# Queries times carried state as one product per head on two row halves, with both heads' outputs in PSUM banks of their own

## The chip, the cores and the metric

The kernel runs on one core of one Trainium2 chip. The core has five engines that run beside each other: TensorE (PE in the profile, its weight loads PEld), VectorE (DVE), ScalarE (ACT), GpSimd (POOL) and SyncE (SP, which issues most transfers). PE writes its results to PSUM, a buffer of eight banks; one bank holds 512 fp32 values on each of 128 partitions. The metric is the device time of one execution in microseconds, lower is better.

## What is computed

One layer of a streaming encoder on 1024 prompt rows and 32 sample rows of width 1024. An input projection feeds two groups of heads, gated linear attention (4 heads, keys of 64, values of 128) and a gMLP; then come an output projection, a normalisation, an MLP of width 4096 with squared ReLU, and a second normalisation. The change lies in the gated attention. The reference computes it block by block, with a matrix state `S` (64 x 128 for each head) that is carried on:

```python
def gla_block(S, q, k, v, g):
    b = jnp.cumsum(g, axis=2)
    o_inter = jnp.einsum('bhid,bhde->bhie', q * jnp.exp(b), S)
    ...
    o = o_inter + jnp.einsum('bhij,bhje->bhie', att, v)
    b_last = b[:, :, -1:, :]
    S_new = jnp.exp(b_last[:, :, 0, :])[..., None] * S + jnp.einsum(
        'bhjd,bhje->bhde', k * jnp.exp(b_last - b), v)
    return S_new, o
...
o = o * lax.rsqrt(jnp.mean(jnp.square(o), axis=-1, keepdims=True) + RMS_EPS) * gla_norm_g.astype(f32)
o_gla = o.reshape(Bn, T, GLA_WIDTH).astype(h.dtype) * jax.nn.silu(r)
```

`o_inter` is the product of queries and carried state that the change touches; everything is in fp32.

## The kernel before

The 1056 rows are cut into three blocks and each block into three windows: eight windows of 128 prompt rows and one of 32 sample rows. The four heads are worked on as two pairs (`Pair`, line 610), one after the other, so 18 windows pass through the attention stage. A pair's two heads lie on top of each other: key dimension of head 0 on partitions 0 to 63, of head 1 on 64 to 127. The state tile `st` (line 615) is 128 x 2 x 128; head 0 fills the rows 0 to 63 of the first 128 columns, head 1 the rows 64 to 127 of the second, and the rest is zero.

For each window, in the generator `gla` (line 860):

- `elem` (line 730) prepares one window ahead the decayed queries and keys, in a tile `zx` of which there are two. POOL, ACT and DVE work on it. The queries that meet the state are `x[:, 3]`.
- `gram` (line 770) multiplies keys and queries in many small products into the PSUM tile `gt` (two banks), transposes the decayed keys (line 793), and puts the masked result into `att`.
- `outp` (line 808) first forms the state's increment (line 817). Then it takes a PSUM tile `o` of one bank, of which there are two in turn (line 819). In its columns 0 to 255 it multiplies queries with the state in one product of 128 rows and 256 columns (line 821; the first window of a pair has none, as its state is zero), and adds `att` times values for each head (line 824). DVE then updates the state (line 830).
- `gla_norm` (line 837) works in two pieces. The first: ACT squares and sums the output (line 844), POOL forms the scale (lines 845 and 846), ACT scales the output into `on` (line 848). The second, due 8000 ns later by the planner's clock (line 849): PE transposes `on` into the columns 256 to 511 of the same `o` (line 851), and DVE multiplies that into `mix` (line 854).

PE's instructions run in the order in which the program writes them (`manual_schedule`, line 104); the other engines' orders are chosen by the framework, which also puts in the waits. The order of writing comes from a planner, `Order` (line 51): generators give back how much PE time a step takes and how long they rest, and the planner takes the stream of the highest priority that is due. `outp` is written, its `gla_norm` is added at priority 0 (line 879) and so its first piece is written at the planner's next step, ahead of the next `gram`, unless an older `gla_norm` is due first. Steps of the projections (`proj_v`, `proj_qk`, `out_proj`, priority 6) fill the time between.

PSUM holds in this stage four banks for `mm` (projections, line 583), two for `gt` and two for `o`: all eight.

Of the kernel before, what the change touches and what calls it, by code (L numbers as in the profile page):

```python
# [10 lines left out]
F32 = mybir.dt.float32  # L11
# [8 lines left out]
P = 128  # L20
# [77 lines left out]
def build(tc, io):  # L98
    nc = tc.nc
    V, S, G, PE, DM = nc.vector, nc.scalar, nc.gpsimd, nc.tensor, nc.sync  # L100
    order = Order()
    ctx = ExitStack()
    with ctx:
# [9 lines left out]
        def mm():  # L113
            return cur["ps"].tile([P, 512], F32, tag="mm", name="mm", bufs=cur["mm"])
# [4 lines left out]
        ident = cst.tile([P, P], F32, name="ident")  # L119
# [6 lines left out]
        def col(name, k, n=1):  # L126
            o = PV[name][0]
            return pv[:, o + k:o + k + n]
# [186 lines left out]
        with tc.tile_pool(name="pa", bufs=1, reuse_waits="tile") as pa, \  # L315
# [36 lines left out]
            for _ in range(3):  # L352
                t = wp.tile([P, 2, 1088], F32, tag="whl", name="wst2", bufs=3)
# [227 lines left out]
        with tc.tile_pool(name="pb", bufs=1, reuse_waits="tile") as pb, \  # L581
# [226 lines left out]
            def outp(pr, b, wi, zx, ak):  # L808
                off, w, c = WIN[b][wi]
                z, x, el = zx  # L810
                att, ks = ak
                vt = pr.v[3 * b + wi]
                st = pr.st[c]
                first = (c == 0 and b == 0 and wi == 0)
                ds = mm()
                for hd in range(2):
                    PE.matmul(ds[64 * hd:64 * hd + 64, :128], ks[:w, 64 * hd:64 * hd + 64],
                              vt[:w, 128 * hd:128 * hd + 128], start=True, stop=True, tile_position=(0, 64 * hd))
                ot = psb.tile([P, 512], F32, tag="o", name="o", bufs=2)
                if not first:  # L820
                    PE.matmul(ot[:w, 0:256], x[:, 3, :w], st.rearrange("p h f -> p (h f)"), start=True, stop=False)
                for hd in range(2):
                    fs_ = slice(128 * hd, 128 * hd + 128)
                    PE.matmul(ot[:w, fs_], att[:w, hd, :w], vt[:w, fs_], start=first, stop=first or hd == 1)
                for hd in range(2):
                    r = slice(64 * hd, 64 * hd + 64)
                    if first:
                        V.tensor_copy(st[r, hd], ds[r, :128])
                    else:
                        V.scalar_tensor_tensor(st[r, hd], st[r, hd], el[r], ds[r, :128], ALU.mult, ALU.add)  # L830
                    if c == 1 or (b == 2 and wi == 1):
                        s0 = 128 * pr.p + 64 * hd
                        DM.dma_start(io["st_s" if c else "st_p"][s0:s0 + 64], st[r, hd])
                pr.out += 1
                return ot

            def gla_norm(pr, b, wi, ot):

                off, w, _ = WIN[b][wi]
                ms = sm.tile([P, 2], F32, tag="ms", name="ms")  # L840
                on = pb.tile([P, 2, 128], F32, tag="on", name="on", bufs=2)
                ov = [ot[:w, 128 * hd:128 * hd + 128] for hd in range(2)]
                for hd in range(2):
                    S.activation(on[:w, hd], ov[hd], AF.Square, accum_out=ms[:w, hd:hd + 1])
                G.tensor_scalar(ms[:w], ms[:w], 1.0 / 128, RMS_EPS, ALU.mult, ALU.add)
                an = [G.tensor_tensor(ms[:w], ms[:w], mhalf[:w].to_broadcast([w, 2]), ALU.pow).ins]
                for hd in range(2):
                    an.append(S.activation(on[:w, hd], ov[hd], AF.Identity, scale=ms[:w, hd:hd + 1]).ins)
                yield 0, 8000
                for hd in range(2):  # L850
                    PE.transpose(ot[:, 256 + 128 * hd:256 + 128 * hd + w], on[:w, hd], ident[:w, :w])
                mx = mix[b][:, 2 * pr.p:2 * pr.p + 2, off:off + w]
                tv = ot[:, 256:512].rearrange("p (h t) -> p h t", h=2)[:, :, :w]
                an.append(V.scalar_tensor_tensor(mx, tv, col("gla_norm_g", 0), mx, ALU.mult, ALU.mult).ins)
                behind[3 * b + wi] = an
                yield 220, 2000
                if wi == 2:
                    pr.normed += 1

            def gla(pr):  # L860
                nxt = None
                for b in range(3):
                    for wi in range(3):
                        if nxt is None:
                            yield lambda: len(pr.dd) >= 1 and len(pr.q) >= 1 and (not pr.p or prs[0].out >= 8)
                            nxt = elem(pr, 0, 0)
                            yield 0, 4000
                        zx = nxt
                        w = WIN[b][wi][1]
                        ak = gram(pr, b, wi, zx)  # L870
                        j = 3 * b + wi + 1
                        yield (1700 if w == 128 else 1700), 200
                        if j < 9:
                            yield lambda: len(pr.dd) > j // 3 and len(pr.q) > j // 3
                            nxt = elem(pr, j // 3, j % 3)
                        yield 0, 3200
                        yield lambda: len(pr.v) >= j
                        ot = outp(pr, b, wi, zx, ak)
                        order.add(gla_norm(pr, b, wi, ot), 0)
                        yield 1300, 0  # L880
# [126 lines left out]
        with tc.tile_pool(name="pd", bufs=1, reuse_waits="tile") as pd, \  # L1007
# [254 lines left out]
            tv = {k: t.rearrange("p (a k n) -> p a k n", a=2, k=2) for k, t in td.items()}  # L1262
# [458 lines left out]
```

## Time and profile before

| what | value |
|---|---|
| time, median of 3 runs | 1234.48 us (1232.83 to 1236.89) |
| the profiled execution's own time | 1231.84 us |
| its span, first to last instruction | 1230.1 us |
| mean granted TensorE clock | 0.979 of full speed |
| PE busy | 1169.0 us, 95% of the span |
| DVE busy | 918.0 us, 75% |
| ACT busy | 528.9 us, 43% |
| POOL busy | 480.6 us, 39% |

Times inside the profile count from the first instruction. The attention stage takes about 256 to 410 us of the span: its first product of `att` and values starts at 256.6 us, its last transposes at 409.3 us. An fp32 product shows as two records, each with its weight load. Rows of the timeline give start, duration, engine, line of the kernel, operation and tiles; where the engine stood idle before a row, brackets give for how long and what ended it. Rows that give windows list, after the stretch and its length, the busy time and number of instructions of PE, PEld, DVE, ACT and POOL, then the granted clock, the share of DMA and GB/s.

### The profile page before, as it was taken

The numbers are of one execution on the slowest core, as the hardware profiler recorded it, in microseconds if no ns is written. First come the engines' busy times: TensorE is split into PE (matmuls) and PEld (weight loads), VectorE is DVE, ScalarE is ACT, GpSimd is POOL, SyncE is SP. The second block draws the span as 40 slices with busy tenths as digits, with TensorE's granted clock in tenths as the row PEclk, the third lists the DMA queues.
The fourth block names the chain that finished last, engine by engine and source line by source line (L and its number), as shares of the span: only waits on it lengthen the run. The fifth ranks groups of instructions, "written<-read, shape, count | busy, mean of one in ns | idle before, by whom it ended". The sixth has DMA issues, their size and how long they took to land.

```text
span 1230.1 us, 22225 instructions
## 1 busy us (share of the span) xinstructions
PE 1169.0 (95%) x8539; PEld 1113.4 (91%) x8539; DVE 918.0 (75%) x1889; ACT 528.9 (43%) x1081; POOL 480.6 (39%) x666
## 2 busy tenths in 40 slices
PE   5999998999899999899989999999999999999994
PEld 3678997988788999789989999999999999999994
DVE  5664797468987688657759769589498696796686
ACT  4462423445555666552435343343443443433221
POOL 3442132246665154358541442334314413432043
PEclk9999998999899999889989999999999999999998
DMA  9631563110102765204762672744825626637412
GB/s 372 240 122 57 194 221 126 35 36 4 39 2 89 263 205 175 101 31 148 267 240 70 206 253 90 256 155 134 300 87 196 242 90 214 227 108 248 141 50 93
DMA packets 49498, 188.46 MB, mean 153 GB/s; under 512 B 5328, under 2 KB 10928, under 8 KB 49392
## 3 DMA queue, kind: packets, MB, share of 16 engines
q1 hardware_dynamic: 35280, 109.97, 25.8%
q0 software_dynamic: 14112, 77.08, 18.2%
q8 instruction: 67, 1.10, 0.4%
q14 instruction: 39, 0.32, 0.1%
HBM read 171.36 MB, written 15.66 MB: 152 GB/s over the span
## 4 chain that ended last, share of the span: by engine, by line
PE 67%; DVE 16%; DMA 5%; POOL 4%; issue 3%; ACT 3%; SPq 0%; POOLq 0%; DVEq 0%; ACTq 0%
PE mm L250 19%; PE mm L1379 15%; PE mm L1446 12%; PE mm L1240 8%; PE mm L284 3%; DVE hl L1043 3%; PE zp L284 2%; DVE jk L903 2%; DMA raw<-in_w_dram 2%; DVE acc L1471 1%; DMA wst<-in_w_dram 1%; DVE wad L903 1%; PE zp L250 1%; DMA tdT<-hl 1%; PE mm L1146 1%
## 5 line engine op out<-in xcount | busy, mean ns | idle before, releaser
L1042 ACT CAST hl<-raw 128x512 fp32r<-128x512 f32 (+1 forms) x238 | 143.8, 613 | 243.5 <-PE mm L1446 95.0
L1043 DVE TENSOR_TENSOR hl<-raw,hl 128x512 fp32r<-128x512 f32 (+1 forms) x238 | 206.0, 871 | 40.7 <-ACT hl L1042 40.7
L1379 PE MATMUL mm<-ring,hl 128*128 128x384 f32 x960 | 173.6, 338 | 3.4 <-DMA ring<-tdT 3.4
L1379 PEld LDWEIGHTS mm<-ring,hl 128*128 128x128 f32 x960 | 168.9, 190 | 3.8 <-issue 3.7
L1446 PE MATMUL mm<-ring,hl 128*128 128x384 f32 x792 | 140.7, 335 | 1.3 <-DVE acc L1471 1.3
L1446 PEld LDWEIGHTS mm<-ring,hl 128*128 128x128 f32 x792 | 137.4, 188 | 1.9 <-ACT ring L1042 1.4
L250 PE MATMUL mm<-hT,whl 128*128 128x384 f32 (+1 forms) x792 | 129.4, 322 | 0.8 <-ACT mix L306 0.8
L250 PEld LDWEIGHTS mm<-hT,whl 128*128 128x128 f32 x792 | 127.0, 188 | 2.2 <-issue 1.1
L250 PE MATMUL mm<-h,hl 128*128 128x288 f32 (+1 forms) x756 | 121.4, 316 | 2.5 <-POOL h L239 2.2
L250 PEld LDWEIGHTS mm<-h,hl 128*128 128x128 f32 x756 | 114.6, 195 | 5.3 <-POOL h L239 4.1
L1087 POOL TENSOR_TENSOR raw<-raw 128x512 f32<-128x512 f32 x26 | 36.3, 1397 | 183.4 <-DMA raw<-in_w_dram 158.8
L1471 DVE SCALAR_TENSOR_TENSOR acc<-mm,G,acc 128x384 f32<-128x384 f32 x162 | 93.6, 606 | 5.3 <-PE mm L1446 4.8
L1240 PE MATMUL mm<-fb,hl 128*128 128x288 f32 x708 | 97.0, 295 | 0.0
L1240 PEld LDWEIGHTS mm<-fb,hl 128*128 128x128 f32 x708 | 95.4, 188 | 0.0
L1251 DVE SCALAR_TENSOR_TENSOR acc<-mm,G,acc 128x256 f32<-128x256 f32 (+3 forms) x176 | 61.6, 389 | 12.2 <-PE mm L1240 12.2
L250 PE MATMUL mm<-mhl,hl 128*128 128x384 f32 (+1 forms) x384 | 63.8, 319 | 2.0 <-ACT hl L1042 1.8
L250 PEld LDWEIGHTS mm<-mhl,hl 128*128 128x128 f32 x384 | 58.8, 188 | 2.6 <-ACT hl L1042 2.1
L1327 POOL DMA_DIRECT2D ring<-tdT x56 | 31.3, 560 | 75.4 <-PE mm L1379 41.3
L284 PE MATMUL mm<-whl,hT 128*128 128x272 f32 (+1 forms) x384 | 54.2, 304 | 5.3 <-DVE whl L637 5.3
L284 PEld LDWEIGHTS mm<-whl,hT 128*128 128x128 f32 x384 | 52.3, 206 | 6.8 <-DVE whl L637 5.5
L284 PE MATMUL zp<-zvw,hT 128*128 128x512 f32 x192 | 53.2, 419 | 4.6 <-ACT hT L236 4.5
L1403 DVE TENSOR_TENSOR tmps<-mm,tmps 128x384 f32<-128x384 f32 x28 | 15.6, 558 | 50.6 <-PE mm L1379 50.6
(255 smaller groups left out, 2246.7 us busy)
## 6 DMA issues: line engine op xcount, KB each, us to landing
ring<-tdT POOLq DMA_DIRECT2D x56, 768.0 KB, 5.7
raw<-in_w_dram SPq DMA_DIRECT2D x80, 512.0 KB, 4.0
ring<-tdB POOLq DMA_DIRECT2D x42, 768.0 KB, 6.3
wst<-in_w_dram SPq DMA_DIRECT2D x34, 512.0 KB, 4.0
wad<-in_w_dram SPq DMA_DIRECT2D x24, 512.0 KB, 4.3
tdT<-hl SPq DMA_DIRECT2D x16, 384.0 KB, 2.7
st<-in_w_dram SPq DMA_DIRECT2D x10, 512.0 KB, 10.2
tdB<-h SPq DMA_DIRECT2D x6, 768.0 KB, 4.5
```

Of the source, the lines that this page charges most:

```text
L250: PE.matmul(pt[:, :n], h[:, a, 128 * kk:128 * kk + 128], act[:, b_, k, :n], start=(i == 0 and j == 0), stop=(i == 7 and j == 2))
L284: PE.matmul(pt[:n, :width], act[:, a, k, off:off + n], hl[:, b_, width * kk:width * kk + width], start=(k == 0 and a + b_ == 0), stop=(k = ...
L903: V.scalar_tensor_tensor(jk, w, 1.0, csb[:, c], ALU.mult, ALU.mult, accum_out=acc_)
L1042: S.copy(hl[:, 0, :n], src)
L1043: V.tensor_tensor(hl[:, 1, :n], src, hl[:, 0, :n].bitcast(F32), ALU.subtract)
L1087: G.tensor_tensor(s, a21, a22, ALU.add)
L1240: PE.matmul(pt[:, :n], hl[kk // 2][:, a, o_:o_ + 128], f(kk)[:, c_], start=(kk == 0 and j == 0), stop=(kk == 3 and j == 2))
L1251: V.scalar_tensor_tensor(ac, pt[:, o + lo - p0:o + hi - p0], G2[:, m, c:c + 1], ac, ALU.mult, ALU.add)
L1327: G.dma_start(s, td[t, j].rearrange("p (a c) -> p a c", a=2))))
L1379: PE.matmul(pt[:, :384], hl[:, a, o_:o_ + 128], quad(ts[j])[:, b_, kk], start=first and j + kk + i == 0, stop=j + kk + i == 4, skip_group_ ...
L1446: PE.matmul(pt[:, :384], hl[:, a, o_:o_ + 128], f[:, b_, kk], start=first and kk + i == 0, stop=kk + i == 3, skip_group_check=True)
L1471: V.scalar_tensor_tensor(ac, v, G2[:, m, 0:1], ac, ALU.mult, ALU.add)
```

## The change

Only `outp` and `gla_norm` change. One PSUM tile `o` of two banks, taken once, serves all 18 windows. Head 0's output lies in its first bank and head 1's in its second. Windows alternate between the left and the right 256 columns of both banks (`half`); of these the first 128 hold the output and the next 128 its transpose. A set, `o_used`, asserts while the program is written that a half is not taken again before its window's second norm piece is written.

The state product becomes one product for each head, of 64 rows and 128 columns: head 0 on the upper row half of the array, head 1 on the lower (`tile_position`), each into its head's bank. The products of `att` and values, the norm's reads and the transposes keep their form and move to the new places.

```diff
-                ot = psb.tile([P, 512], F32, tag="o", name="o", bufs=2)
+                if not o_t:
+                    o_t.append(psb.tile([P, 2, 512], F32, name="o"))
+                half = ocount[0] % 2
+                ocount[0] += 1
+                assert half not in o_used
+                o_used.add(half)
+                ot = o_t[0][:, :, 256 * half:256 * half + 256]
                 if not first:
-                    PE.matmul(ot[:w, 0:256], x[:, 3, :w], st.rearrange("p h f -> p (h f)"), start=True, stop=False)
+                    for hd in range(2):
+                        r = slice(64 * hd, 64 * hd + 64)
+                        PE.matmul(ot[:w, hd, :128], x[r, 3, :w], st[r, hd], start=True, stop=False,
+                                  tile_position=(64 * hd, 0))
                 for hd in range(2):
-                    fs_ = slice(128 * hd, 128 * hd + 128)
-                    PE.matmul(ot[:w, fs_], att[:w, hd, :w], vt[:w, fs_], start=first, stop=first or hd == 1)
+                    PE.matmul(ot[:w, hd, :128], att[:w, hd, :w], vt[:w, 128 * hd:128 * hd + 128], start=first, stop=True)
...
-                return ot
+                return ot, half
...
-                ov = [ot[:w, 128 * hd:128 * hd + 128] for hd in range(2)]
+                ot, half = ot
+                ov = [ot[:w, hd, :128] for hd in range(2)]
...
-                    PE.transpose(ot[:, 256 + 128 * hd:256 + 128 * hd + w], on[:w, hd], ident[:w, :w])
+                    PE.transpose(ot[:, hd, 128:128 + w], on[:w, hd], ident[:w, :w])
                 mx = mix[b][:, 2 * pr.p:2 * pr.p + 2, off:off + w]
-                tv = ot[:, 256:512].rearrange("p (h t) -> p h t", h=2)[:, :, :w]
+                tv = ot[:, :, 128:128 + w]
                 an.append(V.scalar_tensor_tensor(mx, tv, col("gla_norm_g", 0), mx, ALU.mult, ALU.mult).ins)
                 behind[3 * b + wi] = an
+                o_used.remove(half)
```

More of the change, by code (lines that the diff above doesn't have):

```diff
@@ L834, in outp @@
                 pr.out += 1
-                return ot
+                return ot, half
+            o_t, ocount, o_used = [], [0], set()
             def gla_norm(pr, b, wi, ot):
```

## The prediction, made before the changed kernel was run

> **What bounds the kernel now.** I read the page first: the busy digits of TensorE (PE) by slice, the granted clock, and the chain that ended last.
>
> ```profile
> span 1230.1 us, 22225 instructions
> ...
> PE   5999998999899999899989999999999999999994
> ...
> PEclk9999998999899999889989999999999999999998
> ...
> PE 67%; DVE 16%; DMA 5%; POOL 4%; issue 3%; ACT 3%; SPq 0%; POOLq 0%; DVEq 0%; ACTq 0%
> ```
>
> One slice is 30.75 us, so the gated-attention stage, 256 to 410 us, is slices 8 to 13, counted from 0. PE is nearly full there and carries two thirds of the chain. PE's order is written by hand (line 104), so whatever makes PE wait holds back all PE work behind it. Next I read the timeline of one undisturbed cycle, from one window's attention product (L824) to the next one's:
>
> ```profile
> 343.24 0.70 PE L821 MATMUL o<-st,zx 128*128 128x256 f32 x2
> 343.77 0.61 PE L824 MATMUL o<-v,att 128*128 128x128 f32 x4
> 344.02 0.40 POOL L741 TENSOR_TENSOR zx<-b 128x128 f32<-128x128 f32 x1 [10.67 <-PE o L821]
> 344.31 0.46 PE L783 MATMUL gt<-zx 64*32 64x32 f32 x32
> 344.59 0.26 ACT L844 ACTIVATE on<-o 128x128 f32<-128x128 f32 x1
> ...
> 344.99 0.20 ACT L844 ACTIVATION_READ_ACCUMULATOR on<-o 128x1 f32 x1
> ...
> 345.84 0.33 PE L793 MATMUL mm<-ident,zx 128*128 128x128 f32 x1
> 346.01 0.38 PE L851 MATMUL o<-ident,on 128*128 128x128 f32 x2
> 346.14 4.53 PE L284 MATMUL mm<-whl,hT 128*128 128x256 f32 x36
> 346.43 0.48 DVE L854 SCALAR_TENSOR_TENSOR mix<-o,pv,mix 128x256 f32<-128x256 f32 x1
> 346.79 0.29 POOL L749 TENSOR_TENSOR zx<-b 128x64 f32<-128x64 f32 x1
> 347.04 0.46 POOL L764 TENSOR_TENSOR zx<-zx,q 128x128 f32<-128x128 f32 x1
> 347.58 0.21 POOL L845 TENSOR_SCALAR ms<-ms 128x2 f32<-128x2 f32 x1
> 348.29 0.69 POOL L846 TENSOR_TENSOR ms<-ms,mhalf 128x2 f32<-128x2 f32 x1
> 349.02 0.63 ACT L848 ACTIVATE on<-o,ms 128x128 f32<-128x128 f32 x2 [1.02 <-POOL ms L846]
> 350.60 0.44 PE L817 MATMUL mm<-v,ks 128*64 128x128 f32 x4
> 350.97 0.70 PE L821 MATMUL o<-st,zx 128*128 128x256 f32 x2
> 351.51 0.27 PE L824 MATMUL o<-v,att 128*128 128x128 f32 x1
> ```
>
> The columns are start, duration, engine, line. Call the window whose L824 starts at 343.77 **new** and the one before it **old**. PE computes the new output (L821, L824), the gram products of the next window (L783 to L793), transposes the old window's normalised output (L851, 346.01), and then fills the rest with 36 projection matmuls (L284). Meanwhile ACT squares the new output (L844), POOL first works off the next element block (L741 to L764) and only then forms the scale (L845, L846), and ACT scales the new output (L848), which ends at 349.02 + 0.63 = 349.65. That is 5.88 us after the new L824 began; the old window's L851 began 2.24 us after it. Today this order costs nothing: old and new lie in different banks and different buffers. The cycle takes 351.51 - 343.77 = 7.74 us.
>
> **The change part by part.** *The state product.* L821 is one product of 128 rows and 256 columns, issued as two records; from its start to L824 is 351.51 - 350.97 = 0.54 us. It becomes four records of 64 rows and 128 columns, on two row halves.
>
> ```profile
> L821 PE MATMUL o<-st,zx x32: 379/391/483, 264.6 to 398.5; 128*128 128x256 f32 x28, 128*32 128x256 f32 x4
> ```
>
> That is 32 / 2 = 16 products, one for each window but the first of each pair. No row shows such a half-row product. The nearest is L817: four records on two column halves, 350.97 - 350.60 = 0.37 us to the next group. The four full-array records of L824 take 344.31 - 343.77 = 0.54. So a product costs 0.37 if its halves run side by side, 0.54 if they do not, and at worst 0.71 with one more rearrangement of the array, estimated at the 0.17 by which the two differ. I take 0.37, the row of the same form: 16 x (0.37 - 0.54) = **-2.7 us**; the other ends are 0 and +2.7. The added weight loads are inside these starts.
>
> *The PSUM tile.* Before, each window had its own tile of one bank, two taking turns. After, one tile of two banks serves all windows: head 0 in the first bank, head 1 in the second, and windows alternate between the left and right 256 columns. Old and new window never share columns, but they now share both banks and one tile. Does the program order accesses of different engines to one tile when their data do not meet? The trace has such a pair: L233 (DVE) and L236 (ACT) both only read the same PSUM tile and write different buffers.
>
> ```profile
> L233 DVE TENSOR_SCALAR t<-mm,a,c x64: 296/590/679, 18.4 to 529.0; 128x384 f32<-128x384 f32 x32, 128x256 f32<-128x256 f32 x16, 128x32 f32<-128x32 f32 x16
> ...
> L236 ACT ACTIVATE hT<-mm,c,a x32: 362/618/672, 19.0 to 84.0; 128x384 fp32r<-128x384 f32 x16, 128x256 fp32r<-128x256 f32 x8, 128x32 fp32r<-128x32 f32 x8
> its engine sat idle before it (us, times) until:
>   DVE t L233: 40.3, 22
> ```
>
> ACT idled 40.3 us in 22 waits on a mere reader of the same bank. So I take it that any two engines on one bank of one tile are put in program order. The Trainium skill, page "PSUM — Partial Sum Buffer", section "PSUM bank collisions raise a hardware error", says that two engines touching one bank in the same 32 partitions collide even at disjoint columns and even when both read, so such pairs must be ordered; the trace agrees, with those 40.3 us. By that page the wait below must arise; a rule by bytes alone would leave the sum at -2.7.
>
> *The wait that follows.* A window's first norm piece (L838 to 848) is written right after its output (line 879, priority 0), before the next gram. PE's rows show L851 of the old window after that gram. Hence the old L851, a PE write to both banks, stands in program order behind the new window's L848, an ACT read of both banks. PE would wait at L851 from 2.24 to 5.88 us after L824: **3.64 us per cycle**. Behind it on PE queue the 36 projection matmuls, then L817, L821 and L824 of the next window; behind those, POOL's next element block (freed by L821), and the whole stage. Nothing hides the wait: PE has no other work allowed past it. The new cycle is 5.88 + (351.51 - 346.01) = 11.38 us. The opposite wait, an output (L821) behind the old window's L854, costs nothing: L854 begins 0.42 us after L851, and some 4.5 us of projections lie between.
>
> ```profile
> 265.11 0.61 PE L824 MATMUL o<-v,att 128*128 128x128 f32 x4
> 275.04 0.38 PE L851 MATMUL o<-ident,on 128*128 128x128 f32 x2
> 275.35 0.46 PE L783 MATMUL gt<-zx 64*32 64x32 f32 x32
> 398.83 0.62 PE L824 MATMUL o<-v,att 32*32 32x128 f32 x4
> 400.55 0.38 PE L851 MATMUL o<-ident,on 128*128 128x128 f32 x2
> 401.15 0.61 ACT on L848 x2
> ```
>
> From the second window's L824 to the last one's there are 16 cycles in 398.83 - 265.11 = 133.7 us. In one (275.04) L851 comes straight after L824 and before the gram, so it is written ahead of the new norm piece and does not wait. The other 15 do. 15 x 11.38 + 7.74 = 178.4, which is +44.7 over 133.7; this lets the longer cycle absorb the 133.7 - 16 x 7.74 = 9.9 us of other waits that the stage has now. After the last output one more L851 waits from 400.55 to 401.76: +1.2. Together **+45.9 us**.
>
> *The clock.* PE would now stand idle 3.64 us per cycle.
>
> ```profile
> 322.70 4.55 PE L284 MATMUL mm<-whl,hT 128*128 128x256 f32 x36
> ...
> 332.39 0.44 PE L783 MATMUL gt<-zx 64*32 64x32 f32 x16 [3.32 <-DVE zx L762]
> ...
> 336.07 6.87 PE L284 MATMUL mm<-whl,hT 128*128 128x256 f32 x36
> ```
>
> ```profile
> 329.10:332.40 3.30, 0.01 (x2) 0.01 (x2) 3.30 (x3) 1.23 (x7) 3.21 (x5) 0.80 0.00 0
> 332.40:341.30 8.90, 8.90 (x89) 7.49 (x90) 8.03 (x35) 2.81 (x8) 0.88 (x1) 0.50 0.01 2
> ...
> 629.30:632.60 3.30, 0.00 (x0) 0.00 (x0) 2.14 (x2) 0.41 (x1) 3.26 (x4) 0.83 0.91 333
> 632.60:638.20 5.60, 5.53 (x17) 5.50 (x18) 1.31 (x3) 0.62 (x1) 2.40 (x4) 0.50 1.09 422
> ```
>
> The column after the engines is the granted clock. Both times that PE idled about 3.3 us, 5.6 to 8.9 us at half clock followed, and 36 projection matmuls took 6.87 us instead of 4.55: 2.3 us more. Stalls of 3.64 us should do the same, though not surely each: at half clock the gram runs longer and eats into the next stall. I charge two thirds of the 16: 11 x 2.3 = **+25 us**; the ends are 0 and 16 x 2.3 = 37. The Trainium skill, page "TensorE: Matmul & The Clock Gate", part 1, puts the threshold at an idle window of about 3.4 us; the 3.3 us rows agree roughly. By that page every stall would halve the clock and the sum would be 12 us higher.
>
> **Sum:** -2.7 + 45.9 + 25 = +68 us. The profiled execution took 1231.84 us (1.7 around its span of 1230.1); the median shown is 1234.48. So 1300 on the profiled run, and **1302 us** against the median.
>
> **The rivals.** *No wait arises* (not slower). If order is kept by bytes, not by banks, old and new window stay independent through their column halves; this decides all, from the first L851 on. Then only the state product counts: 1234.5 - 2.7 = about 1232, within 0.3%. For it: the two windows' columns never meet. Against: 40.3 us of ACT behind a reader. Chance 0.08, of which 0.03 beyond 0.3% faster.
>
> *The scale is formed early.* POOL's order is not written by hand. If L845 and L846 go ahead of the element block, L848 ends sooner: after the last window, where no block stands in the way, 401.76 - 398.83 = 2.93 us. The stall is then 0.7 us, 15 x 0.7 = 10, less up to 9.9 absorbed and 2.7 for the product: 1232 to 1242. Against: in the cycle shown POOL runs the block from L741 to L764 before L845 (347.58), although ACT had delivered at 344.99 + 0.20, 2.4 us earlier, and nothing in the change gives POOL a reason to reorder. Chance 0.10.
>
> *The halves do not run side by side:* the first term is 0 or +2.7, which changes no sign; it is in the range.
>
> **How the numbers follow.** The forecast, a PE stall of some 2.5 to 4 us in nearly every cycle, with or without half clock, has 0.82. Its own range: at the low end a stall of 2.5 us, 15 x (2.5 - 3.64) = -17 on +43 and no half clock, +26: 1260. At the high end all 16 at half clock (+37), nothing of the 9.9 absorbed and the product at +2.7: 2.7 + 45.9 + 37 + 9.9 = +96: 1330, and ten more for cycles in which ACT or POOL are late as well: 1340. The range 1254 to 1340 holds about 0.8. A measurement here tells 0.3% (3.7 us) from no change. Faster 0.03; within 0.3% 0.09 (0.05 of the first rival, 0.04 of the second); slower 0.88.
>
> **What would show it.** Right: L851 becomes one of PE's largest waiters, released by ACT L848, 3 to 4 us some 15 times; cycles from L824 to L824 near 11 us; granted clock well under 1.0 between 265 and 450 us; everything after the stage shifted, not slower. The half-row product should take 0.37 us to the next group. Wrong: L851 follows the gram without a gap while ACT L848 of the newer window comes later (no order by bank); or L845 stands directly behind L844 (POOL reordered); or stalls without a drop of the clock, which takes 25 us off.

## The result, and the profile after

The changed kernel takes 1307.22 us (median of 5 runs, 1304.72 to 1308.14) against 1233.86 us for the kernel before in the same comparison: ratio 1.059, 95% interval 1.057 to 1.061. It is 73 us slower; forecast were 68 us, 1302 us, and a range of 1254 to 1340. The profiled execution took 1307.84 us, its span is 1306.1.

The page of the changed kernel: span, PE's busy tenths, granted clock in tenths, and the chain that ended last by engine.

```profile
span 1306.1 us, 22312 instructions
...
PE   5999998986866789989998999999999999999995
...
PEclk8999998987777789998999999999999999999998
...
PE 76%; DVE 9%; POOL 5%; DMA 3%; ACT 3%; issue 2%; SPq 0%; DVEq 0%; ACTq 0%; POOLq 0%
```

A slice is now 32.65 us. The stage of gated attention fills slices 8 to 14, counted from 0: PE fell to 6 to 8 tenths there and the clock to 7 to 8 tenths. Outside these slices the two pages look alike. The view of waits names the culprit in its first row (columns: who waited, for whom; us in total, times, longest):

```profile
PE o L863 <- ACT on L860: 54.6, 16, 6.8
```

The lines have moved: L863 is the transposes (L851 before), L860 the scaling on ACT (L848 before), L829 and L832 are the state product and the product of `att` and values (L821 and L824 before). Before, the transposes stood in no row of this view. Now a cycle of the changed kernel, for the same windows as the one shown of before (start, duration, engine, line):

```profile
387.94 0.49 PE L829 MATMUL o<-st,zx 64*128 64x128 f32 x4
...
388.36 0.71 PE L832 MATMUL o<-v,att 128*128 128x128 f32 x4
...
388.54 0.40 POOL L741 TENSOR_TENSOR zx<-b 128x128 f32<-128x128 f32 x1 [10.19 <-PE o L829]
...
389.00 0.46 PE L783 MATMUL gt<-zx 64*32 64x32 f32 x32
389.11 0.27 ACT L856 ACTIVATE on<-o 128x128 f32<-128x128 f32 x1
...
390.53 0.33 PE L793 MATMUL mm<-ident,zx 128*128 128x128 f32 x1
...
392.09 0.21 POOL L857 TENSOR_SCALAR ms<-ms 128x2 f32<-128x2 f32 x1
...
392.80 0.69 POOL L858 TENSOR_TENSOR ms<-ms,mhalf 128x2 f32<-128x2 f32 x1
...
393.52 0.63 ACT L860 ACTIVATE on<-o,ms 128x128 f32<-128x128 f32 x2 [1.01 <-POOL ms L858]
...
394.20 0.69 PE L863 MATMUL o<-ident,on 128*128 128x128 f32 x2 [3.34 <-ACT on L860]
...
394.54 6.84 PE L284 MATMUL mm<-whl,hT 128*128 128x256 f32 x36
...
394.99 0.48 DVE L866 SCALAR_TENSOR_TENSOR mix<-o,pv,mix 128x256 f32<-128x256 f32 x1 [0.16 <-PE o L863]
...
401.68 0.49 PE L829 MATMUL o<-st,zx 64*128 64x128 f32 x4
...
402.10 0.71 PE L832 MATMUL o<-v,att 128*128 128x128 f32 x4
```

Read it from L863 upwards. It transposes the older window, whose data have been ready for a cycle. It starts at 394.20, 0.05 us after ACT has scaled the newer window (393.52 + 0.63). PE stood idle for 3.34 us in front of it. The 36 projection matmuls behind it take 6.84 us; in the cycle of before, 36 such matmuls took 4.53. The cycle from L832 to L832 is 402.10 - 388.36 = 13.74 us instead of 7.74.

Two rows of windows, the first of the changed kernel and the second of before, over the cycles from the second window to the last (busy time of the engines, then the granted clock, here 0.77 and 0.96):

```profile
265.10:477.50 212.40, 158.95 (x1803) 138.54 (x1802) 117.45 (x433) 80.18 (x280) 78.98 (x227) 0.77 0.07 24
```

```profile
265.00:400.00 135.00, 129.40 (x1779) 111.63 (x1778) 115.60 (x435) 77.88 (x284) 81.98 (x227) 0.96 0.12 37
```

The stage grew from 133.7 us to 212.4, by 78.7; the span grew by 76.0. So the loss arises in the stage, and what follows made up less than 3 us of it. DVE, ACT and POOL have the same work as before. PE's busy time grew by some 30 us, which fits the half clock, and its idle time from 5.6 to 53.5 us. The granted clock in these traces is either 1.00 or 0.50, so 0.77 on average means half clock for 2 x (1 - 0.77) = 46% of the stage, 98 us; before it was 2 x 0.04 x 135 = 11 us.

### The profile page after: what moved, and what is told of

Its sections match the earlier page's. It is cut to its first block, busy times and chain, and to the rows that moved or that the text cites. A ratio compares the mean times of both kernels' runs of the same rounds, so it can differ in the third digit from the quotient of the medians.

```text
span 1306.1 us, 22312 instructions
## 1 busy us (share of the span) xinstructions
PE 1198.4 (92%) x8571; PEld 1138.5 (87%) x8571; DVE 922.3 (71%) x1889; ACT 531.5 (41%) x1081; POOL 477.1 (37%) x666
## 4 chain that ended last, share of the span: by engine, by line
PE 76%; DVE 9%; POOL 5%; DMA 3%; ACT 3%; issue 2%; SPq 0%; DVEq 0%; ACTq 0%; POOLq 0%
PE mm L250 24%; PE mm L1392 15%; PE mm L1253 12%; PE mm L1459 11%; PE mm L284 4%; PE zp L284 2%; DVE jk L916 2%; POOL zx L748 1%; POOL zx L749 1%; DVE acc L1484 1%; DMA ring<-tdT 1%; DVE hl L1056 1%; DMA wst<-in_w_dram 1%; PE mm L1159 1%; PE zp L250 1%
## 5 line engine op out<-in xcount | busy, mean ns | idle before, releaser
L1459 PE MATMUL mm<-ring,hl 128*128 128x384 f32 x792 | 140.7, 335 | 1.2 <-DVE acc L1484 1.1
L250 PE MATMUL mm<-hT,whl 128*128 128x384 f32 (+1 forms) x792 | 139.4, 339 | 1.0 <-ACT mix L306 1.0
L250 PEld LDWEIGHTS mm<-hT,whl 128*128 128x128 f32 x792 | 137.0, 202 | 3.0 <-issue 1.6
L284 PE MATMUL mm<-whl,hT 128*128 128x272 f32 (+1 forms) x384 | 62.6, 334 | 5.3 <-DVE whl L637 5.3
L284 PEld LDWEIGHTS mm<-whl,hT 128*128 128x128 f32 x384 | 61.0, 239 | 6.8 <-DVE whl L637 5.5
L863 PE MATMUL o<-ident,on 128*128 128x128 f32 (+1 forms) x36 | 10.4, 385 | 54.6 <-ACT on L860 54.6
```

What stands on the lines that cost most here:

```text
L250: PE.matmul(pt[:, :n], h[:, a, 128 * kk:128 * kk + 128], act[:, b_, k, :n], start=(i == 0 and j == 0), stop=(i == 7 and j == 2))
L284: PE.matmul(pt[:n, :width], act[:, a, k, off:off + n], hl[:, b_, width * kk:width * kk + width], start=(k == 0 and a + b_ == 0), stop=(k = ...
L1459: PE.matmul(pt[:, :384], hl[:, a, o_:o_ + 128], f[:, b_, kk], start=first and kk + i == 0, stop=kk + i == 3, skip_group_check=True)
```

## The experiments

The theory is that of the prediction: the program orders ACT's read of the newer window ahead of PE's write of the older, because they share two banks of one tile; PE's hand-written order passes the wait on to everything; and the idle time halves the clock. The main rival is that the row halves themselves cost the time. Two questions more: how much of the loss is the clock, and what sets the length of the stall.

### e1: the layout without the row halves

```diff
-                        PE.matmul(ot[:w, hd, :128], x[r, 3, :w], st[r, hd], start=True, stop=False,
-                                  tile_position=(64 * hd, 0))
+                        PE.matmul(ot[:w, hd, :128], x[:, 3, :w], st[:, hd], start=True, stop=False)
```

> The changed kernel with its PSUM tile as it is, but the state product of each head on the full 128 rows (the other head's rows of the state are zero), so without the row halves. Theory (the shared banks put L863 behind the newer window's L860): the stall stays, 16 waits of about 3.4 us, and each product takes 0.54 instead of 0.42 us to L832: 1307 + 16 x 0.12 = 1309 us. Rival (changing the array between column halves, row halves and the full array costs the time): no row halves, no loss, about 1234 us.

Measured: 1313.42 us, ratio 1.065 (1.062 to 1.068). The view of waits of e1, where L861 is the transposes:

```profile
PE o L861 <- ACT on L858: 56.1, 16, 6.8
```

The same 16 waits stand there without any row halves. The rival falls: the layout alone brings the whole loss, and the row halves do not add to it. That e1 is 6 us over the changed kernel, where 2 were expected, stays unexplained beyond the stall's 1.5 us.

### e11 and e12: the norm piece behind the transposes

This moves one thing. A window's first norm piece waits, in the order of writing, until the older window's transposes are written. The planner's due times are kept, and PE's instructions stand in the same order as in the changed kernel.

```diff
+                mine, due = begun[0], order.now + 8000.0
+                begun[0] += 1
+                yield lambda: turned[0] >= mine
...
-                yield 0, 8000
+                yield due
+                turned[0] += 1
```

> The changed kernel with one thing moved: the newer window's norm piece is written right behind the older window's transposes instead of ahead of them. PE's instructions stand in the same order as in the change, and the planner's times are kept. Theory (only the order of that pair on the shared banks matters): no wait at the transposes, no half clock beyond that of before, stage back to 134 us, and the cheaper product left: 1232. Rival (something else of the change costs, and e4 and e8 hid it by moving projections): 1240 or more.

> Control for e11: the kernel before with the norm piece written behind the older transposes, PE's order as before. Theory: 1234, no difference from before; e11 less e12 is the product, -2 us, which five rounds may just show. Rival: the late norm piece costs by itself, and both lie above 1238.

Measured: e11, on the changed kernel, 1235.25 us, ratio 1.0031 (1.0017 to 1.0045). e12, on the kernel before, 1233.22 us, ratio 0.9999 (0.9985 to 1.0014). PE's waits in the stage of e11 (L829 and L832 are the output products):

```profile
PE o L829 <- ACT on L865: 4.7, 4, 1.6
PE o L832 <- ACT on L865: 3.1, 1, 3.1
```

No transposes are left in the view. Of 73 us all but 2.7 are gone, with the shared banks, the row halves and PE's order all as in the change. So it was the order of writing of the norm piece's reads on ACT and the transposes' writes on PE. What is left is the same rule from the other side: five times an output now waits, 7.8 us together, for the scaling of the window before, which has become later.

Two parts of the expectation did not come. The row of windows from e11's second output to its last is:

```profile
264.90:405.60 140.70, 132.74 (x1803) 114.98 (x1801) 112.72 (x433) 78.57 (x280) 83.25 (x227) 0.92 0.11 36
```

The stage takes 140.7 us and not 134, and half clock takes some 2 x 0.08 x 140.7 = 23 us of it against 11 before; most of the 7 us is made up behind the stage. Why the half clock grew was not tested. And the 2 us that the product should bring do not show: e11 lies 2 us over e12, not under it. The part on the prediction says why there was nothing to bring.

### e4, e5, e8 and e9: two other orders of writing

An earlier attempt at the same order: the transposes are written directly behind the newer output, ahead of the gram, and the norm's rest is cut to 5500 ns.

```diff
+                yield lambda: turned[0] >= mine
...
-                yield 0, 8000
+                yield 0, 5500
+                yield lambda: prs[0].out + prs[1].out in (mine + 2, 18)
+                turned[0] += 1
```

> The changed kernel with another order of writing: the older window's transposes are written right behind the newer output, and the newer norm piece behind them, so that no PE write stands behind an ACT read of the newer window. Banks are shared as in the change. Theory: L863 no longer waits, L856 waits about 1 us for the older window's DVE read, which nobody needs soon; only the cheaper product is left, 16 x 0.12 = 2 us: 1232 against 1234 before. Rival (sharing two banks costs by itself, whatever the order): 1250 or more.

> The kernel before with that same other order of writing: control for e4. Theory: no wait to remove, so 1234, within 0.3%; e4 less e5 is the product alone, about -2 us. Rival (the order is better or worse by itself): a difference from 1234 that e4 shares.

Measured: e4 1234.62 us, ratio 1.0007 (0.9993 to 1.0022); its control e5, the same order on the kernel before, 1238.1 us, ratio 1.0032 (1.0015 to 1.0048). Sharing the banks costs nothing measurable when no PE write stands behind a late read. PE's largest wait in e4, in the window from 256 to 490 us:

```profile
PE mm L250 <- ACT hl L1062: 8.4, 1, 8.4
```

This lies behind the stage, where PE waits for the next stage's first weights: more projections had been pulled into the cycles, so PE came to that place early in its order and stood there. e8 and e9 were to mend that with one projection step less in each cycle (the rest behind the gram 0 instead of 200 ns).

> e4 with one step of projections less in each cycle (the rest behind the gram is 0 instead of 200 ns of the planner), because e4's stage took 144.9 us from the second window's L832 to the last one's instead of 133.7, with PE waiting 8.4 us for the next stage's weights afterwards. Theory: no stall, cycles near 7.6 us, and of the stage's length only the cheaper product counts: 1232, 2 us under before. Rival (with fewer projections between, the gram waits for POOL's element block): PE waits at L783 instead, and 1234 or more.

> Control for e8: the kernel before with e8's order of writing. Theory: e8 plus 2 us, about 1234. Rival: the same waits at L783 as e8, and then both lie over before by the same amount.

Measured: e8 1236.64 us, ratio 1.0025 (1.0009 to 1.0041); e9 1236.64 us, ratio 1.0029 (1.0013 to 1.0044). A miss: both lie 0.3% over before, and they do not differ. The rival's waits at L783 did not come either (0.2 us in e8). In e8 too the product takes 0.42 us at PE, but the group behind it starts later by nearly what that saves, as the part on the prediction works out for the changed kernel. No version beat the kernel before.

### e6 and e7: banks of their own for each window

```diff
-            cur["ps"], cur["mm"] = psb, 4
+            cur["ps"], cur["mm"] = psb, 2
...
-                ot = o_t[0][:, :, 256 * half:256 * half + 256]
+                ot = psb.tile([P, 2, 512], F32, tag="o", name="o", bufs=2)[:, :, 0:256]
...
-                yield from out_proj_first()
-                yield from out_proj(0, 2)
+                yield from out_proj(0)
```

e7 is the kernel before with the first and last of these edits.

> The row halves with banks of their own for each window too: two tiles of two banks in turn instead of one, paid for with two banks fewer for projections (2 instead of 4 mm tiles); the first two output projections are therefore written one after the other. Theory: no stall at L863 in spite of the row halves and the old order of writing; e6 less e7 is the product alone, about -2 us. Rival (row halves cost by themselves): e6 is tens of us over e7.

> The kernel before with 2 instead of 4 mm tiles in the attention stage and the first two output projections one after the other: control for e6. Theory: slower than before by waits of PE for evictions; the granted size is not known, between 0 and some 40 us.

Measured: e6 1242.76 us, ratio 1.0076 (1.0049 to 1.0103); e7 1242.95 us, ratio 1.0078 (1.0055 to 1.0101). PE's waits of e6, largest first:

```profile
PE gt L783 <- DVE zx L762: 4.2, 4, 3.3
PE mm L227 <- ACT xr L1196: 3.7, 1, 3.7
PE mm L817 <- DVE v L681: 2.8, 1, 2.8
```

In the old order of writing, with row halves, and with both heads in separate banks, the transposes wait no more, since the older and the newer window have different tiles again. The price is the two projection tiles, 9 us with or without the row halves. So it is the sharing between windows, not the splitting between heads. e6 gives back both the tile and the banks, so it does not tell which of the two sets the order.

### e2: filling the stall

```diff
+                if begun[0] > turned[0]:
+                    dt = mm()
+                    for _ in range(11):
+                        PE.matmul(dt[:, :128], ones, ident, start=True, stop=True)
                 for hd in range(2):
                     PE.transpose(ot[:, hd, 128:128 + w], on[:w, hd], ident[:w, :w])
```

> The changed kernel with 11 added 128 x 128 fp32 products, which nobody reads, ahead of the transposes of the older window where the newer norm piece is written first. At 4 records in 0.54 us they take about 11 x 0.27 = 3.0 us, inside the stall of 3.4. Theory (the stall also halves the clock): PE is kept at work, the granted clock stays at 1.00 in the stage, and the time falls although work is added, by some 25 us, to about 1282. Rival 1 (the half clock costs nothing, as the cycle is set by POOL): 1307, no change. Rival 2 (PE was not idle in the stall): 1307 + 16 x 3.0 = 1355.

Measured: 1290.97 us, ratio 1.047 (1.044 to 1.050). The wait at the transposes (L871), and the stage's row of windows:

```profile
PE o L871 <- ACT on L862: 21.3, 11, 4.3
```

```profile
265.00:457.90 192.90, 171.58 (x2135) 153.12 (x2132) 117.01 (x433) 80.34 (x280) 81.02 (x227) 0.94 0.09 27
```

PE does 16 x 11 products more, and the kernel is 16 us faster. The clock rose from 0.77 to 0.94, and half clock fell from 98 to 2 x 0.06 x 192.9 = 23 us. The fall is smaller than the 25 us expected, since a quarter of the half clock stayed and since some stalls are shorter than their filling. Both rivals fall.

### e3 and e10: a shorter stall, and the same one filled

In e3 POOL may begin a window's element block only behind the scale of the last norm piece written.

```diff
+                es = ExitStack()
+                if scale_ins[0] is not None:
+                    es.enter_context(tc.issue_after(scale_ins[0]))
                 G.tensor_tensor(x[:, 2, :w], last.to_broadcast([P, w]), bb, ALU.subtract)
...
+                es.close()
...
+                scale_ins[0] = an[0]
```

> The changed kernel, but the element block of a window (from L741) may go on POOL only behind the scale of the last window whose norm piece was written. Theory (the stall's length is POOL's block ahead of the scale): L860 ends about 3.1 us after L832 instead of 5.8, the stall shrinks to about 1 us, the clock stays up; 16 x 1 = 16 over the time before, less 2 for the product and less some waits that the longer cycle covers: 1240 to 1250 us. If the element blocks, now about 1 us later, hold up the next gram, up to 16 more. Rival (L863 waits for something else of the newer window than its scaling): stalls of 3 us and 1300 or more stay.

Measured: 1263.91 us, ratio 1.024 (1.021 to 1.028). Waits at the transposes (L870), one cycle on PE, and the stage's row of windows:

```profile
PE o L870 <- ACT on L867: 21.1, 16, 2.8
```

```profile
292.09 0.33 PE L799 MATMUL mm<-ident,zx 128*128 128x128 f32 x1
293.30 0.44 PE L870 MATMUL o<-ident,on 128*128 128x128 f32 x2 [0.88 <-ACT on L867]
...
294.51 4.96 PE L250 MATMUL mm<-hT,whl 128*128 128x384 f32 x18
```

```profile
266.60:437.50 170.90, 148.47 (x1802) 128.15 (x1800) 116.18 (x434) 78.25 (x280) 80.78 (x227) 0.84 0.09 30
```

The stall shrank as expected, 54.6 to 21.1 us with 0.88 us as the common value, so its length is POOL's block ahead of the scale. But the time stayed 14 us above the expected 1240 to 1250. The last row gives the likely reason: the clock is 0.84, so half clock still takes 2 x 0.16 x 170.9 = 55 us, though only one of the 16 stalls reaches 2.5 us. e10 tests that with 5 filling products per stall (the diff of e2 with 5 for 11).

> e3 with 5 added 128 x 128 products, which nobody reads, ahead of the older window's transposes: 5 x 0.22 = 1.1 us in stalls of 0.9 to 2.8. Theory (what e3 keeps over the time before is mostly half clock: 54.6 us of it in the stage, in 10 stretches, although most stalls were only 0.9 us): the half clock goes, worth 54.6 x 0.28 = 15 us by e2's rate, less some 2 us of products that outlast their stall: 1264 - 13 = about 1251. Rival (e3's rest is the stall itself and later element blocks): 1264 or more.

Measured: 1246.64 us, ratio 1.011 (1.008 to 1.013). Waits (transposes are L878) and the stage, which in e10 runs from 264.3 to 414.3 us:

```profile
PE o L878 <- ACT on L869: 4.8, 5, 1.8
```

```profile
264.30:414.30 150.00, 142.66 (x1952) 124.86 (x1950) 114.23 (x434) 78.74 (x280) 81.49 (x227) 0.99 0.11 34
```

17 us less than e3, by added work; the clock is back at 0.99. Filling adds about as much PE time as it covers, so by this reckoning what went is half clock: 52 us of it, worth a third of its length. The rival falls.

## Why the prediction was right, step by step

**The wait by bank** was the step on which all hung, and the wait was right: 16 waits of PE for ACT, 54.6 us, at the line named. The one cycle that was to have none (its transposes follow L832 directly) has none. The prediction had 15 times 3.64 us in the cycles and 1.2 us behind the last, 55.8. That the totals lie so close is partly luck. Seven waits have the common 3.34 us, which is the forecast one: the transposes start 5.84 - 2.24 = 3.60 us later than before, and the view counts from the end of L793. Five are shorter (1.1 to 2.6 us), where POOL has less or nothing ahead of the scale, and four longer (4.5 to 6.8 us), where the transposes stand ahead of the gram or POOL has more to do. e11 shows the cause with PE's order unmoved. The rival without a wait falls with it: columns that never meet were put in order.

That the order goes *by bank* is not shown, since old and new window share a tile as well. In the cycle shown, L863 starts behind both scalings of L860 (393.52 + 0.63). Its first transpose writes head 0's bank alone, and head 0's scaling, the first of the two at some 0.36 us each, had ended about 0.3 us earlier. That looks like an order by tile, or like one wait for both; no run separates these.

**The cycle.** The cycle shown became 13.74 us. The prediction's 11.38 at full clock plus 2.3 for a half-clock filling gives 13.68.

**The stall and the clock** were right in kind and both a little small. Added up over the 16 cycles of the two timelines, PE comes 50.9 us later to the transposes, counted from the L832 ahead of them, and takes 27.7 us longer from the transposes to the next L832: together the stage's growth. The first is the stall, where 44.7 us were forecast. The second is the clock's part, where 25 were forecast for 11 of 16 stalls; in the trace half clock falls behind the transposes in all 15 cycles with a stall, and not in the one without. The experiments agree roughly: of the 98 us at half clock, 87 are more than before, and by e2 (16 us for 75 us less, some of it taken by the filling) and e3 with e10 (17 for 52) they cost an estimated 19 to 28 us.

**The trigger of the half clock** was mis-sized. The prediction took it from idle times of 3.3 us. In e3, three of the seven stalls of 0.85 to 0.89 us were followed by it within 2 us. That mattered little for the forecast, where most stalls were long anyway, but it made the second rival's price wrong. With the scale formed early the prediction had 1232 to 1242 us. e3, which forces that, measured 1264; its stalls too were longer than that rival's, 21 us together instead of 10. POOL did not reorder by itself in the changed kernel: L857 still runs 3.7 us behind L832.

**The product** is the term that was wrong, though it is small. It was sized at 0.37 us by L817, the nearest row, and takes 402.10 - 401.68 = 0.42 instead of 0.54; so the two halves seem to run beside each other. But the group behind it, L832, whose form did not change, now takes 389.00 - 388.36 = 0.64 us to the gram; L824 took 344.31 - 343.77 = 0.54. From the state product to the gram it is 1.06 us after and 1.07 before. What the halves save, the next group gives back, so the term is about 16 x 0.01 = 0.2 us and not 2.7. The prediction, and the theories of e1, e4, e6, e8 and e11 after it, priced a product up to the next group's start and no further. In e1, e4, e6 and e8, each beside its partner, the time differed by 6, 3.5, 0.2 and 0.0 us in favour of the row halves, and in e11 by 2 us against them; with 0.2 us at stake, these differences are not the product's. What holds L832 up by 0.10 us was not tested.

**What was absorbed.** The prediction took off 9.9 us as other waits that the longer cycle covers. They were not all waits: PE's idle time in these cycles before was 5.6 us, and the rest is cycles with more work or at half clock. The 3.32 us wait at L783 is indeed gone from the view, and its cycle is the only one that became clearly shorter, by 2.2 us. Of the 15 x 3.64 = 54.6 us of forecast stall 50.9 came, so 3.7 us were absorbed and not 9.9. Stall, clock and product were thus too low by some 6, 3 and 2.5 us. That the span still grew only 8 us more than the 68 forecast is in part because 3.8 us, counted with the last wait, were made up behind the stage, where the sum had assumed none.

## What to carry to other kernels

Before two buffers of a rotating pair are put into one PSUM tile, look at which engine touches the newer one between the older one's last uses: data that never met were still put in order here, and an engine with a fixed order turns that wait into a stall of everything behind it. The cure need not be more banks. Writing the late reader behind the early writer took away 71 of 73 us here, with PE's instructions in the same order. A PE stall can cost more than its length, as the clock falls with it: 55 us of waits brought 73 us. And price a new form of product up to the start of the group after the next, since what it saves may be given back there: here 0.12 us saved, 0.10 given back.

## What the runs showed of the hardware

The half clock does not need the idle time that the prediction supposed. In e3, three of seven stalls of about 0.88 us behind a gram were followed by it, and four were not. In e7 it came with hardly any idle time; rows of windows, with PE's busy time first and the granted clock third from the end:

```profile
289.37:292.78 3.41, 3.27 (x84) 2.23 (x71) 2.66 (x11) 2.05 (x10) 3.25 (x13) 1.00 0.02 5
292.78:296.20 3.42, 3.42 (x12) 3.04 (x11) 3.25 (x16) 2.28 (x7) 1.04 (x2) 0.50 0.01 2
296.20:300.00 3.80, 3.80 (x88) 3.01 (x87) 3.67 (x12) 1.78 (x10) 1.62 (x6) 1.00 0.00 0
```

PE's timeline in the first of these stretches begins with the gram and ends so:

```profile
290.86 0.38 PE L851 MATMUL o<-ident,on 128*128 128x128 f32 x2
291.38 0.91 PE L703 MATMUL mm<-glr,wg 16*128 16x384 f32 x2
292.21 4.39 PE L250 MATMUL mm<-hT,whl 128*128 128x384 f32 x14
```

PE was busy 3.27 of 3.41 us there, but with the gram's small products, transposes and a product of 16 rows; projections fill only the last 0.57 us. The next 3.42 us ran at half clock. So a stretch of some 3.4 us with little done in the array seems to be enough, whether PE idles or works on small tiles; this is one stretch, not a rule. The Trainium skill, page "TensorE: Matmul & The Clock Gate", part 1, describes a free-running window of that length and an idle one as the trigger; the length agrees with the 3.4 us stretch, but here an idle window was not needed. Which share of the array's work keeps the clock up was not measured. It would explain why 11 plain 128 x 128 products in a stall paid for themselves.
